# One ring of four raw weight buffers in the MLPs, loaded from SyncE three blocks ahead, and the third up tile in two single PSUM banks

## The chip, the cores and the metric

The kernel runs on one core of one Trainium2 chip. Its time is the device time of one execution, in microseconds; the figure that counts is the median of several runs. A core has five engines that work through their instructions in order and meet at semaphores: TensorE (PE in the profile; its weight loads are listed as PEld), VectorE (DVE), ScalarE (ACT), GpSimd (POOL) and SyncE (SP). Data lie in HBM, in the on-chip SBUF, and, for what TensorE writes, in the eight banks of PSUM. DMA transfers are issued by an engine (here ScalarE or SyncE) and carried by 16 DMA engines.

## What is computed

One inference step of a two-layer streaming encoder over 576 tokens (512 of a new stream and 64 of a running one), with a model width of 1024 and an MLP width of 4096. Layer 0 mixes tokens by causal pooling, layer 1 by sparse attention; each is followed by the same kind of MLP. Cut to what the change touches:

```python
def _rmsnorm(x, g):
    xf = x.astype(jnp.float32)
    xf = xf * lax.rsqrt(jnp.mean(xf * xf, axis=-1, keepdims=True) + EPS)
    return (xf * g.astype(jnp.float32)).astype(x.dtype)

def _mlp(h, w_up, w_down):
    u = jax.nn.relu(h @ w_up)
    return (u * u) @ w_down

...
for i in range(DEPTH):
    h = _rmsnorm(x, norm_mix[i])
    ...
    x = x + y.astype(x.dtype)
    x = x + _mlp(_rmsnorm(x, norm_mlp[i]), mlp_w_up[i], mlp_w_down[i])
```

## The kernel before

**Stages.** Four stages follow one another: the pooling mixer (about 0 to 47 us of the span), the first MLP (48 to 457), the attention (457 to 761) and the second MLP (761 to the end). Each opens its own pools of SBUF and PSUM tiles (`stage`, L65, with the buffer counts that the calls at the file's end give); a tile of a new stage waits until the old tiles at its place have been read.

**Activations and products.** The residual `x` is kept transposed, as 8 tiles of 128 features by 576 tokens. Every fp32 value is split into a high part and a rest, and a product takes three matmuls: high by high, high by rest, rest by high. A matmul has weights of 128x128 and 288 tokens, half of the 576. An up tile (`project`, L226 to L234) is 128 hidden features by 576 tokens: 8 weight slices x 3 x 2 halves = 48 matmuls into a tile of two PSUM banks (`psum("up")`, of which the stage has two, `ps=2`). Single banks come from `psum1`, of which there are four (`po=4`).

**Weights.** All weight blocks go in one fixed order, the list `jobs` (L130 on). The generator `made` (L170) takes the next job: a `block` is 128x1024 fp32 (512 KB), loaded by `load` (L123 to L126) into one of two tiles of the pool `raws`, from ScalarE's DMA queue, and split into two *units* of 128x512 (`split_unit`, L164 to L168): ScalarE casts the high part `wh` (L166), VectorE (GpSimd for the first tiles of an MLP) subtracts for the rest `wl` (L167). Units lie in a ring of six, and within the MLPs two more, every fourth one. `next_unit` (L200) hands the oldest one to the matmuls and keeps up to five made ahead.

**Down products.** The 4096 hidden features go in four chunks, `c` = 0 to 3. All four chunks of the first MLP and the first three of the second use Strassen-like products with 7 instead of 8 products per `Pair` (L359): two blocks of `w_down` (a `pair` job, loaded on ScalarE's queue at L183 into the two tiles of a pool of its own, `pairs`) give seven units, three of them sums that GpSimd makes (L186, L187, L191, L194). TensorE does seven products of 12 matmuls (L356), three (`opening`) into banks a, b and c, then four (`closing`) that go on in banks a, b, c and b. They are read out by ScalarE or VectorE (L379 to L383) and VectorE (L395), each of which adds a bank to `x`. A chunk has four pairs. Before the down products of a chunk the first up tile of the next one is made.

**The norm of an MLP.** `xs` is the unnormed input times the gain; the scale per token comes later. `norm.stats` (L254, matmuls `st` at L284) sums the squares over features, a chain of small operations on ScalarE and VectorE (L301 to L308) gives the inverse root, `norm.spread` (L259) makes a diagonal of it (L274, L277) and spreads it over partitions with matmuls `rb` (L264), which ScalarE copies to SBUF (L265). Then `activated` (L325) reads an up tile, clamps it and scales it (VectorE, L327), ScalarE squares it (L328), and `factors` (L335 to L348) makes the operands `u` of the Strassen products from each two tiles. The loop at L424 on calls it thus:

```python
pt = psum("up")
project(pt, w, xs)
todo.append((c, i, pt, us[c]))
if n == 0:
    norm.stats()
    continue
if n == 1:
    norm.spread()
for t in todo:
    finished(*t)
```

**Order.** Program order is the order of the calls; a scheduler then places instructions on each engine by priorities and dependences, and what it fixes is what the engines execute, in order. In the first MLP TensorE's order is tile, tile, `st`, `rb`, tile; in the second it is tile, `st`, tile, `rb`, tile. The end of the kernel (`last`, L450) and the attention are not touched; the attention ends with `x` plus the output product (L1118) and the second MLP's first up tile takes banks that this addition reads.

Of the kernel before, what the change touches and what calls it, by code (L numbers as in the profile page):

```python
# [16 lines left out]
P = 128  # L17
# [20 lines left out]
UNITS = 6  # L38
# [5 lines left out]
def pool_dsa_kernel(ctx: ExitStack, tc: tile.TileContext, a, o):  # L44
# [5 lines left out]
    weights = ctx.enter_context(tc.tile_pool(name="weights", bufs=UNITS))  # L50
    raws = ctx.enter_context(tc.tile_pool(name="raws", bufs=2))
# [71 lines left out]
    def load(src, n, queue):  # L123
        raw = raws.tile([P, 4 * 264], F32, tag="raw", name=uid("raw"))
        queue.dma_start(raw[:, :n], src)
        return raw  # L126
# [15 lines left out]
    jobs.extend(("block", a["w_in"][j], KT * P) for j in range(2))  # L142
    jobs.extend(("block", a["w_v"][j], 4 * 264) for j in range(2))
    jobs.extend(("block", a["w_in"][j], KT * P) for j in range(2, 15))
    for _ in range(2):
        jobs.extend(("block", a["w_o"][m], KT * P) for m in range(KT))
# [4 lines left out]
    def unit(n=512):  # L151

        extra = phase.get("more")
        count[0] += 1
        if extra and made_units[0] % 4 == 3:
            got = [extra.tile([P, 528], F32R, tag=t, bufs=2, name=uid(t)) for t in ("wh", "wl")]
        else:
            got = [weights.tile([P, 528], F32R, tag=t, name=uid(t)) for t in ("wh", "wl")]
        made_units[0] += 1
        return [t[:, :n] for t in got]  # L160

    made_units = [0]

    def split_unit(src, n=512):  # L164
        h, l = unit(n)
        act.copy(h, src)  # L166
        how["sub"].tensor_tensor(l, src, f32(h), ALU.subtract)  # L167
        return h, l  # L168

    def made():  # L170
# [1054 lines left out]
```

## Time and profile before

| | |
|---|---|
| median of 3 runs | 1180.39 us (1179.42 to 1181.02) |
| profiled execution | 1183.02 us, of which 1181.3 us are the span |
| mean granted clock of TensorE | 0.977 of full |
| raw up blocks, loads | 64 of 512 KB, 3.6 us median from issue to landing |
| DMA | 116.67 MB, 99 GB/s mean; ScalarE's queue 84.45 MB, SyncE's 30.90 MB |
| VectorE's splits (L167) | 139.6 + 101.3 + 70.2 us for raw, pair and sum units |
| GpSimd's sums of a pair | 37.4 + 38.7 + 40.4 + 43.0 us for 28 pairs |

The profile is of one execution. Busy shares are read per engine over the span; an engine's waits are listed by what came last before it went on. A tile name stands for all buffers of that name: `raw`, `pair` and `sum` are fp32 weights, `wh` and `wl` the split ones, `a`, `b`, `c` the banks of a pair, `up` those of an up tile.

### The profile page before, as it was taken

The numbers are of one execution on the slowest core, as the hardware profiler recorded it, in microseconds if no ns is written. First come the engines' busy times: TensorE is split into PE (matmuls) and PEld (weight loads), VectorE is DVE, ScalarE is ACT, GpSimd is POOL, SyncE is SP. The second block draws the span as 40 slices with busy tenths as digits, with TensorE's granted clock in tenths as the row PEclk, the third lists the DMA queues.
The fourth block names the chain that finished last, engine by engine and source line by source line (L and its number), as shares of the span: only waits on it lengthen the run. The fifth ranks groups of instructions, "written<-read, shape, count | busy, mean of one in ns | idle before, by whom it ended". The sixth has DMA issues, their size and how long they took to land.

```text
span 1181.3 us, 20612 instructions
## 1 busy us (share of the span) xinstructions
PE 1117.8 (95%) x8244; PEld 1096.1 (93%) x8244; DVE 811.7 (69%) x1478; ACT 529.9 (45%) x968; POOL 354.4 (30%) x274
## 2 busy tenths in 40 slices
PE   7989989999999999999979999899999999999995
PEld 7989989999999988899878999899989999999995
DVE  7756566666667687658999973856666776775434
ACT  6634334334434434434368665644344334434331
POOL 7700330140132064027675341100430330350002
PEclk8989999999999999999989999999999999999998
DMA  5312232233124125186552332422241233123212
GB/s 170 112 56 67 65 118 72 57 114 99 54 72 143 54 70 192 37 232 195 147 165 69 116 111 79 161 90 61 83 126 55 71 116 99 37 73 116 81 37 80
DMA packets 51151, 116.67 MB, mean 99 GB/s; under 512 B 9345, under 2 KB 22960, under 8 KB 51056
## 3 DMA queue, kind: packets, MB, share of 16 engines
q10 hardware_dynamic: 23184, 84.45, 23.1%
q1 hardware_dynamic: 27872, 30.90, 8.9%
q8 instruction: 65, 1.06, 0.4%
q14 instruction: 30, 0.25, 0.1%
HBM read 99.73 MB, written 13.25 MB: 96 GB/s over the span
## 4 chain that ended last, share of the span: by engine, by line
PE 59%; issue 14%; DVE 14%; POOL 6%; DMA 4%; ACT 3%; SPq 0%; DVEq 0%; ACTq 0%; POOLq 0%
PE up L234 33%; DVE wl L167 6%; PE dn L234 4%; PE b L356 3%; PE o L986 3%; DMA raw<-in_w_up 2%; PE wo L234 2%; PE a L356 2%; PE wa L234 2%; PE c L356 2%; PE sc L947 2%; PE pt L967 1%; POOL sum L194 1%; POOL sum L186 1%; POOL sum L187 1%
## 5 line engine op out<-in xcount | busy, mean ns | idle before, releaser
L234 PE MATMUL up<-xs,wh 128*128 128x288 f32 x2048 | 360.4, 298 | 7.3 <-DVE x L1118 3.4
L234 PEld LDWEIGHTS up<-xs,wh 128*128 128x128 f32 x2048 | 304.6, 191 | 8.8 <-ACT sq L251 4.8
L166 ACT CAST wh<-raw 128x512 fp32r<-128x512 f32 (+1 forms) x210 | 126.6, 619 | 226.1 <-PE up L234 90.8
L234 PE MATMUL up<-xs,wl 128*128 128x288 f32 x1024 | 222.1, 297 | 0.7 <-DVE wl L167 0.7
L167 DVE TENSOR_TENSOR wl<-raw,wh 128x512 fp32r<-128x512 f32 (+1 forms) x186 | 139.6, 756 | 95.2 <-ACT wh L166 93.5
L234 PEld LDWEIGHTS up<-xs,wl 128*128 128x128 f32 x1024 | 166.7, 190 | 1.1 <-DVE wl L167 1.1
L356 PE MATMUL b<-u,wh 128*128 128x288 f32 x672 | 139.1, 300 | 10.2 <-DVE x L395 8.1
L167 DVE TENSOR_TENSOR wl<-pair,wh 128x512 fp32r<-128x512 f32 x112 | 101.3, 910 | 35.9 <-ACT wh L166 35.3
L194 POOL TENSOR_TENSOR sum<-sum,pair 128x512 f32<-128x512 f32 x28 | 43.0, 1534 | 275.9 <-DVE wl L167 275.9
L356 PEld LDWEIGHTS b<-u,wh 128*128 128x128 f32 x672 | 108.1, 190 | 14.3 <-DVE x L395 10.4
L186 POOL TENSOR_TENSOR sum<-pair 128x512 f32<-128x512 f32 x28 | 37.4, 1337 | 274.1 <-DMA pair<-in_w_down 274.1
L166 ACT CAST wh<-sum 128x512 fp32r<-128x512 f32 x84 | 51.0, 620 | 150.4 <-POOL sum L187 44.1
L166 ACT CAST wh<-pair 128x512 fp32r<-128x512 f32 x112 | 68.0, 619 | 90.9 <-PE up L234 40.8
L356 PE MATMUL b<-u,wl 128*128 128x288 f32 x336 | 99.6, 299 | 2.4 <-DVE wl L167 2.3
L327 DVE SCALAR_TENSOR_TENSOR v<-up,rbm 128x576 f32<-128x576 f32 x64 | 48.2, 756 | 73.1 <-PE up L234 70.1
L356 PE MATMUL a<-u,wh 128*128 128x288 f32 x448 | 92.2, 297 | 2.6 <-DVE u L347 2.0
L356 PE MATMUL c<-u,wh 128*128 128x288 f32 x448 | 91.6, 296 | 2.6 <-DVE x L395 2.4
L167 DVE TENSOR_TENSOR wl<-sum,wh 128x512 fp32r<-128x512 f32 x84 | 70.2, 847 | 33.5 <-ACT wh L166 33.2
L234 PE MATMUL pj<-xs,wh 128*128 128x288 f32 x448 | 80.2, 296 | 0.0
L356 PEld LDWEIGHTS a<-u,wh 128*128 128x128 f32 x448 | 72.4, 189 | 3.4 <-DVE u L347 2.3
L356 PEld LDWEIGHTS c<-u,wh 128*128 128x128 f32 x448 | 71.7, 188 | 4.0 <-ACT wh L166 3.3
L234 PEld LDWEIGHTS pj<-xs,wh 128*128 128x128 f32 x448 | 67.3, 190 | 0.7
(229 smaller groups left out, 2218.7 us busy)
## 6 DMA issues: line engine op xcount, KB each, us to landing
raw<-in_w_up ACTq DMA_DIRECT2D x64, 512.0 KB, 3.6
pair<-in_w_down ACTq DMA_DIRECT2D x56, 512.0 KB, 3.6
raw<-in_w_o ACTq DMA_DIRECT2D x16, 512.0 KB, 3.6
raw<-in_w_in ACTq DMA_DIRECT2D x15, 512.0 KB, 4.7
q<-st SPq DMA_DIRECT2D x32, 144.0 KB, 2.6
q<-q SPq DMA_DIRECT2D x16, 256.0 KB, 2.9
raw<-in_w_down ACTq DMA_DIRECT2D x8, 512.0 KB, 3.6
x<-in_x SPq DMA_DIRECT2D x8, 288.0 KB, 6.1
```

The source lines that it names most:

```text
L166: act.copy(h, src)
L167: how["sub"].tensor_tensor(l, src, f32(h), ALU.subtract)
L186: pool.tensor_tensor(s1, a21, a22, ALU.add)
L187: pool.tensor_tensor(s2, s1, a11, ALU.add)
L194: pool.tensor_tensor(s2, s2, a12, ALU.add)
L234: pe.matmul(pt[:, h, :m], wt, xs[k][:, part, c:c + m], start=(k == 0 and i == 0), stop=(k == n - 1 and i == 2),)
L327: dve.scalar_tensor_tensor(v, pt[:, :, :HT], 0.0, halves(norm.rb), ALU.max, ALU.mult)
L356: pe.matmul(bank[:, :HT], wt, ut, start=first and j == 0 and i == 0, stop=last and j == 3 and i == 2, skip_group_check=True)
L947: pe.matmul(pt[:, hh, :nw], q[:, 2 * s + hh], ks[g][:, part, :nw], start=part == 0, stop=part == 1)
L967: pe.transpose(pp[:, c:c + P], pr[:, hh, kt * P:(kt + 1) * P], ident)
L986: pe.matmul(oc[:, 2 * s + hh], pT[:, c:c + P], V[:, kt, vs], start=kt == 0, stop=kt == i)
```

## The change

**One ring.** The pool `pairs` goes. Within an MLP all raw blocks, up and down, take tiles in turn from `raws` (two) and from a further pool of the stage (two), a ring of four. A pair's two blocks are two entries of the list (`even`, `odd`), and its sum a21 + a11 is made in place in the raw tile, as before in the pair's. The sums `s1`, `s2` have a pool of four of their own.

**Loads.** A new generator, `loaded`, issues the loads of up to three blocks before it gives out the first of them (one outside the MLPs). The MLPs' blocks (`up`, `even`, `odd`, `down`) are loaded from SyncE, the others (`w_in`, `w_v`, `w_o`) still from ScalarE.

**Units.** The ring of six and two stays for the MLPs' blocks; the others use the six.

**Third up tile.** `norm.stats` comes after the second tile, `norm.spread` after the third, and the three tiles are then finished together. Since the stage has two double tiles of PSUM, the third tile takes two single banks, and `activated` reads it with two operations of 288 tokens. In the changed program TensorE's order is, in both MLPs, tile, tile, `st`, tile (its matmuls alternating between the two banks), `rb`, tile.

The diff, cut to its core:

```diff
@@ -35,7 +35,10 @@
 NORM_STEPS = (5, 14, 17)
 PACE = (1, 2, 2)
 SLOTS = {"xs": 8, "a": 3, "b": 3, "c": 3, "d": 3, "e": 2}
-UNITS = 6
+UNITS = (6, 2)
+RAWS = (2, 2)
+MLP_BLOCKS = ("up", "even", "odd", "down")
+LOADS_AHEAD = {True: 3, False: 1}
 UP_ORDER = (0, 4, 1, 5, 2, 6, 3, 7)
 FACTORS = ("b11", "b22", "b21", "t1", "t2", "t3", "t4")
@@ -120,8 +123,21 @@
         def __getitem__(self, k):
             return self.t[k // 2][:, k % 2]
-    def load(src, n, queue):
-        raw = raws.tile([P, 4 * 264], F32, tag="raw", name=uid("raw"))
+    turns = {"raw": 0, "unit": 0}
+    def longer(what, sizes, mlp):
+        if not (mlp and "more" in phase):
+            return False
+        t, turns[what] = turns[what], turns[what] + 1
+        return t * sizes[1] // sum(sizes) != (t + 1) * sizes[1] // sum(sizes)
+    def raw_tile(mlp=False):
+        pool = phase["more"] if longer("raw", RAWS, mlp) else raws
+        return pool.tile([P, 4 * 264], F32, tag="raw", name=uid("raw"))
+    def load(src, n, queue, mlp=False):
+        raw = raw_tile(mlp)
         queue.dma_start(raw[:, :n], src)
         return raw
@@ -129,71 +145,71 @@
     def mlp_jobs(layer, strassen):
         for c in range(4):
-            ups = [("block", a["w_up"][layer, c * 8 + f], KT * P) for f in UP_ORDER]
+            ups = [("up", a["w_up"][layer, c * 8 + f], KT * P) for f in UP_ORDER]
             jobs.extend(ups[1:] if c else ups)
             if c < 3:
-                jobs.append(("block", a["w_up"][layer, (c + 1) * 8 + UP_ORDER[0]], KT * P))
+                jobs.append(("up", a["w_up"][layer, (c + 1) * 8 + UP_ORDER[0]], KT * P))
             if c < strassen:
-                jobs.extend(("pair", a["w_down"][layer, c, 2 * q], a["w_down"][layer, c, 2 * q + 1]) for q in range(KT // 2))
+                for m in range(KT):
+                    jobs.append(("odd" if m % 2 else "even", a["w_down"][layer, c, m], KT * P))
             else:
-                jobs.extend(("block", a["w_down"][layer, c, m], KT * P) for m in range(KT))
+                jobs.extend(("down", a["w_down"][layer, c, m], KT * P) for m in range(KT))
...
-    def unit(n=512):
...
+    def unit(n=512, mlp=False):
+        pool = phase["more"] if longer("unit", UNITS, mlp) else weights
+        return [pool.tile([P, 528], F32R, tag=t, name=uid(t))[:, :n] for t in ("wh", "wl")]
+    def split_unit(src, mlp):
+        h, l = unit(src.shape[1], mlp)
         act.copy(h, src)
         how["sub"].tensor_tensor(l, src, f32(h), ALU.subtract)
         return h, l
+    def loaded():
+        waiting = []
+        while jobs or waiting:
+            while jobs and len(waiting) < LOADS_AHEAD["more" in phase]:
+                kind, src, n = jobs.pop(0)
+                mlp = kind in MLP_BLOCKS
+                waiting.append((kind, load(src, n, nc.sync if mlp else act, mlp)[:, :n], mlp))
+            yield waiting.pop(0)
     def made():
-        while jobs:
-            kind, one, two = jobs.pop(0)
-            if kind == "block":
-                raw = load(one, two, act)
+        blocks = loaded()
+        for kind, raw, mlp in blocks:
+            if kind != "even":
+                n = raw.shape[1] // 2
                 for i in range(2):
-                    yield split_unit(raw[:, i * two // 2:(i + 1) * two // 2], two // 2)
+                    yield split_unit(raw[:, i * n:(i + 1) * n], mlp)
                 continue
-            r = [phase["pairs"].tile([P, KT * P], F32, tag="pair", bufs=2, name=uid("pair")) for _ in range(2)]
-            for t, src in zip(r, (one, two)):
-                act.dma_start(t, src)
-            a11, a12, a21, a22 = (t[:, i * 512:(i + 1) * 512] for t in r for i in range(2))
-            s1, s2 = (phase["pairs"].tile([P, 512], F32, tag="sum", bufs=4, name=uid("sum")) for _ in range(2))
+            a11, a12, a21, a22 = (t[:, i * 512:(i + 1) * 512] for t in (raw, next(blocks)[1]) for i in range(2))
+            s1, s2 = (phase["sums"].tile([P, 512], F32, tag="sum", name=uid("sum")) for _ in range(2))
             pool.tensor_tensor(s1, a21, a22, ALU.add)
             pool.tensor_tensor(s2, s1, a11, ALU.add)
-            yield split_unit(a11)
-            yield split_unit(s2)
-            yield split_unit(s1)
+            yield split_unit(a11, mlp)
+            yield split_unit(s2, mlp)
+            yield split_unit(s1, mlp)
             pool.tensor_tensor(a21, a21, a11, ALU.add)
-            yield split_unit(a12)
-            yield split_unit(a21)
+            yield split_unit(a12, mlp)
+            yield split_unit(a21, mlp)
             pool.tensor_tensor(s2, s2, a12, ALU.add)
-            yield split_unit(s2)
-            yield split_unit(a22)
+            yield split_unit(s2, mlp)
+            yield split_unit(a22, mlp)
     units = made()
@@ -232,7 +248,7 @@
             for i, (wt, part) in enumerate(((wh, 0), (wh, 1), (wl, 0))):
                 for h, (c, m) in enumerate(cols):
                     pe.matmul(
-                        pt[:, h, :m], wt, xs[k][:, part, c:c + m],
+                        pt[h][:, :m] if isinstance(pt, tuple) else pt[:, h, :m], wt, xs[k][:, part, c:c + m],
                         start=(k == 0 and i == 0), stop=(k == n - 1 and i == 2),
                     )
@@ -324,7 +340,11 @@
         def activated(pt, v):
-            dve.scalar_tensor_tensor(v, pt[:, :, :HT], 0.0, halves(norm.rb), ALU.max, ALU.mult)
+            if isinstance(pt, tuple):
+                for h in range(2):
+                    dve.scalar_tensor_tensor(v[:, h], pt[h][:, :HT], 0.0, halves(norm.rb)[:, h], ALU.max, ALU.mult)
+            else:
+                dve.scalar_tensor_tensor(v, pt[:, :, :HT], 0.0, halves(norm.rb), ALU.max, ALU.mult)
             act.activation(v, v, AF.Square)
         def plain(pt, u):
@@ -424,13 +444,15 @@
         for n, (c, i) in enumerate(steps):
             if i is not None:
                 w = next_block(sub=add if n < 2 else dve)
-                pt = psum("up")
+                pt = (psum1("up"), psum1("up")) if n == 2 else psum("up")
                 project(pt, w, xs)
                 todo.append((c, i, pt, us[c]))
                 if n == 0:
+                    continue
+                if n == 1:
                     norm.stats()
                     continue
-                if n == 1:
+                if n == 2:
                     norm.spread()
                 for t in todo:
                     finished(*t)
@@ -1120,11 +1142,11 @@
     x = Residual()
     with stage(slots=1, xs=1, tmps=6, ps=3, po=2):
         pool_mixer()
-    with stage(u=1, xs=1, acts=1, tmps=3, pairs=1, more=2, ps=2, po=4):
+    with stage(u=1, xs=1, acts=1, tmps=3, sums=4, more=2, ps=2, po=4):
         mlp(0, 1, 4, pool)
     with stage(slots=1, xs=1, cst2=1, tmps=6, ps=3, po=2):
         attention()
-    with stage(xs=1, u=1, acts=1, tmps=3, pairs=1, more=2, ps=2, po=4):
+    with stage(xs=1, u=1, acts=1, tmps=3, sums=4, more=2, ps=2, po=4):
         mlp(1, 3, 3, end=last)
 
```

More of the change, by code (lines that the diff above doesn't have):

```diff
@@ L131, in mlp_jobs @@
         for c in range(4):
-            ups = [("block", a["w_up"][layer, c * 8 + f], KT * P) for f in UP_ORDER]
+            ups = [("up", a["w_up"][layer, c * 8 + f], KT * P) for f in UP_ORDER]
             jobs.extend(ups[1:] if c else ups)
             if c < 3:
-                jobs.append(("block", a["w_up"][layer, (c + 1) * 8 + UP_ORDER[0]], KT * P))
+                jobs.append(("up", a["w_up"][layer, (c + 1) * 8 + UP_ORDER[0]], KT * P))
             if c < strassen:
-                jobs.extend(("pair", a["w_down"][layer, c, 2 * q], a["w_down"][layer, c, 2 * q + 1]) for q in range(KT // 2))
+                for m in range(KT):
+                    jobs.append(("odd" if m % 2 else "even", a["w_down"][layer, c, m], KT * P))
             else:
-                jobs.extend(("block", a["w_down"][layer, c, m], KT * P) for m in range(KT))
+                jobs.extend(("down", a["w_down"][layer, c, m], KT * P) for m in range(KT))
     mlp_jobs(0, 4)
-    jobs.extend(("block", a["w_in"][j], KT * P) for j in range(2))
-    jobs.extend(("block", a["w_v"][j], 4 * 264) for j in range(2))
-    jobs.extend(("block", a["w_in"][j], KT * P) for j in range(2, 15))
+    jobs.extend(("w_in", a["w_in"][j], KT * P) for j in range(2))
+    jobs.extend(("w_v", a["w_v"][j], 4 * 264) for j in range(2))
+    jobs.extend(("w_in", a["w_in"][j], KT * P) for j in range(2, 15))
     for _ in range(2):
-        jobs.extend(("block", a["w_o"][m], KT * P) for m in range(KT))
+        jobs.extend(("w_o", a["w_o"][m], KT * P) for m in range(KT))
     mlp_jobs(1, 3)
@@ L149, in pool_dsa_kernel @@
     how = {"sub": dve}
-    def unit(n=512):
[L153 to L165, printed above, removed]
+    def unit(n=512, mlp=False):
[3 more added lines that the diff above has]
+        h, l = unit(src.shape[1], mlp)
         act.copy(h, src)
@@ L811, in split_cache @@
             dve.tensor_copy(t[:, :, TP:], f32(new[:, :, TP:]))
-            raw = raws.tile([P, 4 * 264], F32, tag="raw", name=uid("raw"))
+            raw = raw_tile()
             nc.sync.dma_start(raw[:, :TP], src)
```

4 lines of the change are left out of this document (2 added, 2 removed).

## Prediction

> **What bounds the kernel now.** I read the page's busy row first, then the waits of TensorE, then the chain of work that ended last in the stretches where those waits lie, then a table by stage.
>
> ```profile
> PE 1117.8 (95%) x8244; PEld 1096.1 (93%) x8244; DVE 811.7 (69%) x1478; ACT 529.9 (45%) x968; POOL 354.4 (30%) x274
> ```
>
> TensorE is the bound: of a span of 1181.3 us it lacks only 63.5. Nothing in the change takes a matmul away, so all that it can win lies in those 63.5 us and in stretches at a lower clock. The profiled execution took 1183.02 us, 2.6 above the median of 1180.39; I sum savings on the profile and take them from the median.
>
> ```profile
> PE b L356 <- DVE x L395: 8.1, 8, 2.2
> PE rb L264 <- DVE diag L274: 4.8, 2, 2.7
> PE c L356 <- DVE x L395: 2.4, 3, 1.2
> PE a L356 <- DVE u L347: 2.0, 1, 2.0
> ```
>
> Columns: who waited for whom, us in total, times, the longest. The a, b and c rows are the down products of the MLPs; `x L395` is an accumulation that reads a PSUM bank, so TensorE waits there for a bank to come free. An add of 0.45 us isn't slow in itself; the chain says what it stood behind. It is that of the end of chunk 0 in the first MLP:
>
> ```profile
> 149.77 1.30 POOL sum L186
> 151.14 1.30 POOL sum L187
> ...
> 154.75 1.78 DVE wl L167
> 162.23 4.45 DMA raw<-in_w_up
> 167.03 0.45 DVE x L395
> ```
>
> A weight block is asked for at 162.23, one block ahead, and lands 4.45 us later; its split sits in VectorE's order ahead of the accumulation. So a late load becomes a held PSUM bank. Thirteen us earlier the same chain goes through GpSimd's sums of a pair of blocks. By stretch (start:end, us, then PE, PEld, DVE, ACT and POOL busy, clock, DMA share, GB/s): from the first down phase to the last of the first MLP, one undisturbed up phase, and from the first down phase to the third of the second MLP:
>
> ```profile
> 100.00:457.00 357.00, 343.56 (x2529) 338.20 (x2528) 245.40 (x373) 145.38 (x223) 97.24 (x72) 0.99 0.26 82
> 269.00:320.00 51.00, 51.00 (x386) 51.00 (x387) 34.33 (x52) 23.99 (x33) 1.30 (x1) 1.00 0.27 81
> 831.00:1070.00 239.00, 234.24 (x1749) 231.69 (x1748) 166.80 (x254) 95.90 (x150) 71.67 (x55) 1.00 0.27 84
> ```
>
> The up phase is full: 51.00/386 = 132 ns for a matmul, 6.3 us for an up tile of 48, 11.1 us for a pair of 84. So all that the long stretches lack, 13.44 and 4.76, 18.2 us in sum, they lack in the down phases. Of these 2.0 is the wait on `u L347`, the last factor of a chunk, which the change does not touch; 16.2 are open to it.
>
> **The change, part by part.**
>
> *Loads three blocks ahead from SyncE in a ring of four.* A load takes this long from issue to landing (KB each, median us):
>
> ```profile
> pair<-in_w_down ACTq DMA_DIRECT2D x56, 512.0 KB, 3.6
> ```
>
> In the changed program the two blocks of a pair are asked for when the pair before it begins to be split, about 11.1 us of TensorE's work ahead, and the up blocks behind the last pair wait only for the tiles of the pair before. 11.1 against 3.6 to 4.5 hides the transfer, and GpSimd's first two sums (2.6 us) fit behind it. GpSimd's order also has the next pair's sums ahead of the last sum of the pair at hand. I take as won the waits that follow directly from a load or a pair's first sums. Here they are, the idle time of TensorE in brackets:
>
> ```profile
> 144.11 0.37 PE L356 MATMUL c<-u,wh 128*128 128x288 f32 x1 [0.97 <-DVE x L395]
> 157.04 0.37 PE L356 MATMUL c<-u,wh 128*128 128x288 f32 x1 [1.17 <-DVE x L395]
> 167.53 0.41 PE L356 MATMUL b<-u,wh 128*128 128x288 f32 x1 [1.82 <-DVE x L395]
> 268.85 0.40 PE L356 MATMUL b<-u,wh 128*128 128x288 f32 x1 [2.20 <-DVE x L395]
> 366.73 0.40 PE L356 MATMUL b<-u,wh 128*128 128x288 f32 x1 [0.86 <-DVE x L395]
> 449.69 0.53 PE L356 MATMUL b<-u,wh 128*128 128x288 f32 x2 [1.05 <-ACT wh L166]
> 451.27 0.40 PE L356 MATMUL b<-u,wl 128*128 128x288 f32 x1 [1.05 <-DVE wl L167]
> 874.49 0.41 PE L356 MATMUL b<-u,wh 128*128 128x288 f32 x1 [1.63 <-DVE x L395]
> 971.85 0.40 PE L356 MATMUL b<-u,wh 128*128 128x288 f32 x1 [0.62 <-DVE x L395]
> ```
>
> Sum 11.4 us. The other 4.8 of the 16.2, small waits of 0.1 to 0.5, I leave standing. Bounds: 0 (nothing helps) to 16.2. Two of these places also cost clock, in the stretch that follows:
>
> ```profile
> 166.10:168.20 2.10, 0.67 (x5) 0.68 (x6) 2.10 (x4) 0.06 (x1) 0.46 (x1) 1.00 0.01 4
> 168.20:171.60 3.40, 3.40 (x16) 3.40 (x16) 2.04 (x4) 1.24 (x2) 0.00 (x0) 0.51 0.53 157
> 451.50:454.90 3.40, 3.40 (x16) 3.40 (x16) 3.40 (x6) 1.51 (x4) 3.27 (x3) 0.51 0.00 0
> ```
>
> After a stretch with 0.67 of 2.10 us busy the granted clock is 0.51 for 3.4 us, in which TensorE does 1.7 us of full work. If the waits go, 2 x 1.7 = 3.4 us go with them. The Trainium skill ("TensorE: Matmul & The Clock Gate", Why this matters for your kernels) sets the limit higher: no idle gap over about 3 us. By that page a gap of 1.82 would not drop the clock and the 3.4 would stay. The trace speaks against it here; the rule stands as a rival below.
>
> The issues themselves move from ScalarE's queue to SyncE's, at this price each:
>
> ```profile
> 162.23 0.33 ACTq L125 DMA_DIRECT2D raw<-in_w_up  x1
> ```
>
> ScalarE is 45% busy and was waiting at the places above, so I count nothing. In the MLPs SyncE has nothing else to issue that TensorE waits for; behind a load that waits for its tile stand only later loads, and at the end of the first MLP the attention's reads, which wait for `x L395` anyway.
>
> *The third up tile, and the norm after it.* In the first MLP the sums of squares follow the second tile, and the scale needs them at once:
>
> ```profile
> 65.80:76.10 10.30, 8.41 (x29) 7.33 (x30) 6.03 (x10) 4.69 (x7) 0.00 (x0) 0.50 0.12 47
> 66.31 2.29 PE L264 MATMUL rb<-diag,ones 128*128 128x288 f32 x4 [2.17 <-DVE diag L274]
> 69.97 1.30 PE L234 MATMUL up<-xs,wh 128*128 128x288 f32 x4 [1.37 <-DVE v L327]
> 771.00:782.00 11.00, 9.71 (x71) 9.12 (x70) 5.08 (x14) 3.61 (x9) 0.00 (x0) 1.00 0.36 117
> 779.58 1.13 PE L264 MATMUL rb<-diag,ones 128*128 128x288 f32 x4
> ```
>
> The second MLP already has a tile between the two, and its rows (the last two) are the model: no wait before `rb`, the four matmuls in 1.13 us, clock 1.00. Putting 6.3 us of matmuls into a gap of 2.17 saves the 2.17; `rb` at full clock saves 2.29 - 1.13 = 1.16; and the matmuls from 69.97 to 76.10 run at 0.50, so 3.06 of those 6.13 us come back. Sum 6.4 us. The wait of 1.37 for `v L327` stays in both MLPs, since tiles four and five still take the banks of tiles one and two. The changed program reads the third tile with two operations of 288 columns; an add of that size took 0.45, two of them 0.9, for one tile per MLP, and all of it is hidden since the next product is 6.3 us long. Bounds: if the clock drops all the same, 2.17 to 3.33; for the second MLP 0, as its rows hold no such wait.
>
> *The two entries.* The second MLP starts late, because a load issued at 757.24 holds VectorE:
>
> ```profile
> 764.08 0.76 PE L234 MATMUL up<-xs,wh 128*128 128x288 f32 x4 [3.40 <-DVE x L1118]
> 742.00:761.00 19.00, 18.68 (x128) 18.42 (x126) 18.90 (x27) 12.77 (x22) 5.15 (x3) 1.00 0.43 132
> 743.90 0.68 DVE L167 TENSOR_TENSOR wl<-raw,wh 128x512 fp32r<-128x512 f32 x1
> 743.99 1.74 POOL L186 TENSOR_TENSOR sum<-pair 128x512 f32<-128x512 f32 x1 [24.69 <-DMA pair<-in_w_down]
> 746.28 1.79 DVE L167 TENSOR_TENSOR wl<-raw,wh 128x512 fp32r<-128x512 f32 x1
> 755.22 1.28 DVE L167 TENSOR_TENSOR wl<-raw,wh 128x512 fp32r<-128x512 f32 x2
> ```
>
> In the changed program that load waits for the split that ends at 756.50 (the last row) and not for ScalarE's turn at 757.24, 0.7 us earlier, and GpSimd's three sums, beside which a split took 1.79 instead of 0.68 us (about 3 us lost in all), come later. Against that, up to four more splits (4 x 0.68 = 2.7) are made ahead in a stretch where VectorE is busy 18.90 of 19.00. Net +0.7; bounds -2.7 to +3.4. At the first MLP's start ScalarE makes a few casts earlier among the mixer's scalings: -0.3, bounds -1.5 to 0. Into the attention the first two blocks now wait for tiles of the last pair; they are several split units ahead, so 0, and a load of 3.6 if that cover fails.
>
> **Sum:** 11.4 + 3.4 + 6.4 + 0.7 - 0.3 = 21.6 us. 1180.4 - 21.6 = **1158.8 us** (on the profiled execution 1183.0 - 21.6 = 1161.4).
>
> **The rivals.**
>
> *Half of the waits stay.* VectorE works in order, and GpSimd's adds still slow its splits; banks may be held for that reason with the load long there. For it: the wait of 1.17 at 157.04 has a split of 1.78 just ahead. Against it: those at chunk ends follow loads alone. Then 5.7 + 1.7 + 6.4 + 0 = 13.8: 1166.6, with 1164 to 1171 around it.
>
> *The ring does not do what it says.* Four tiles serve pairs and up blocks alike; if the tiles come free so late that loads are again only just in time, the norm alone is left: 1180.4 - 6.4 = 1174. If that too is eaten at the entries (-2.7, -1.5, -3.6), it is no change. Against it: a tile comes free with the last split of its pair, and the next load has a pair's time.
>
> *The clock does not hang on these gaps.* Two short gaps may stand beside drops that have another cause and stay. Then 21.6 - 3.4 - 3.1 - 1.2 = 13.9: 1166.5. Against it: the norm of the second MLP, with no such gap, kept 1.00. This is the case that the page's rule of 3 us would give.
>
> *Slower: the sums that run ahead meet VectorE all the time.* In a pair VectorE has 7 splits of 0.68 and some 7 accumulations of 0.45: 7.9 us beside 11.1 of TensorE, so 3.2 us of room. Today GpSimd's first sums often run while VectorE waits for the late load. Ahead of time, all four adds of a pair run beside its work. An add beside VectorE's work cost it 1.79 - 0.68 = 1.1 us; four cost 4.4, 1.2 more than the room; over 28 pairs 34 us. It decides from a loss of 3.2 us per pair on: 1158.8 + 34 = 1193. Against it: VectorE is busy 72% of the pair, so about 2.9 adds' worth is met, 3.2 us: just the room. The Trainium skill ("SBUF — State Buffer", Who interferes with whom) says that the port pair which the two share is an exclusive lock and the loser blocks for a whole instruction; worked out from the add of 1.74 above, an estimate, that would be up to 7 us per pair. The trace shows 1.1 for one.
>
> **How the numbers follow.** Forecast as summed (1152 to 1164): 0.50. Half of the waits stay: 0.20. Clock rule: 0.06. Ring late: 0.10, of which 0.04 no change. Slower by VectorE: 0.14, of which 0.01 within the bound. A difference of 0.2% (2.4 us) is about what a measurement of this kernel can tell from no change. So faster 0.82, same 0.05, slower 0.13. The low end is all open terms won: 16.2 + 3.4 + 6.4 + 3.4 = 29.4, 1151; the high end takes in the norm alone, 1174, and an entry lost at 1.5 to 2.7 beside it: 1176. Left out are the slower case and the last of the ring's.
>
> **What would show it.** Right: no `PE rb <- DVE diag` wait in the first MLP and clock 1.00 through its first six tiles; chunk ends without waits for `x L395` behind a load; TensorE's idle time near 50 us (63.5 less 11.4, 2.2 and 0.4). Half right: the same waits, now with a split of over 1 us ahead. Wrong: VectorE's splits in the pairs at a mean over 1.1 us, waits of b and c on `x L395` growing in mid phase; or SyncE's queue waiting for tiles while ScalarE waits for loads; or a new wait where the second MLP starts.

## The result, and the profile after

The changed kernel takes 1142.33 us (median of 4 runs, 1141.16 to 1144.35) against 1180.7 before (4 runs): a ratio of 0.9677 with a 95% interval of 0.9658 to 0.9696, 38 us faster. The forecast was 1158.8 us with a range down to 1151: the sign was right, the size was not, for the gain is 1.8 times the 21.6 us of the sum. The profiled execution took 1141.55 us, its span 1139.8; against the profiled span of before that is 41.5 us, of which some 3 are the spread of single runs (a second profile of the changed kernel has a span of 1142.0).

The page's first row, and those of TensorE's waits (who waited for whom, us, times, longest) in the changed kernel that bear on the change. Lines have moved: `L356` is now `L376`, `L395` is `L415`, `L327` is `L347`, `L264` is `L280`, the split `L167` is `L176`, and GpSimd's sums `L186`, `L194` are `L202`, `L210`:

```profile
PE 1097.8 (96%) x8244; PEld 1083.8 (95%) x8244; DVE 839.9 (74%) x1480; ACT 532.8 (47%) x968; POOL 365.5 (32%) x274
```

```profile
PE ix L901 <- ACT rl L909: 5.1, 3, 2.0
PE up L250 <- DVE v L347: 2.6, 2, 1.3
PE a L376 <- DVE u L367: 2.0, 1, 2.0
PE up L250 <- DVE x L1140: 1.1, 1, 1.1
PE c L376 <- DVE x L415: 0.8, 1, 0.8
PE b L376 <- DVE u L368: 0.6, 1, 0.6
```

The 10.5 us of waits of b and c on `x L395` are down to 0.8. What is left in the MLPs is in the main the wait for the scaled up tile (2.6) and for a chunk's last factors (2.0 and 0.6), the first two of which the prediction had left standing. But TensorE's busy time itself fell by 20.0 us with the same 8244 matmuls, and that was not all clock. Down phases of chunks 1 and 2 of the first MLP, before and after (start:end, us, PE, PEld, DVE, ACT, POOL busy, clock, DMA share, GB/s):

```profile
220.00:269.00 49.00, 46.26 (x343) 45.20 (x342) 32.84 (x55) 16.07 (x28) 20.46 (x15) 1.00 0.31 95
320.00:367.00 47.00, 45.56 (x338) 44.52 (x337) 31.24 (x55) 15.63 (x27) 20.55 (x15) 1.00 0.30 93
```

```profile
207.00:250.00 43.00, 43.00 (x328) 43.00 (x327) 34.22 (x55) 17.16 (x28) 12.56 (x9) 1.00 0.32 108
302.00:345.00 43.00, 43.00 (x327) 43.00 (x326) 34.86 (x56) 17.16 (x28) 12.54 (x9) 1.00 0.36 109
```

After, the down phase is full: 43.00 us busy of 43.00, 131.1 ns for a matmul. Before, it was 46.26/343 = 134.9 ns, at a clock of 1.00. So besides the idle time there was a loss inside the busy time. It isn't a slower pace: from one start to the next a matmul takes 132 ns (median) in both traces. The loss stands at the waits. A matmul is listed with 0.29 us (the profile models its end) although the next one starts 0.13 us after it, so the first 0.16 us of every wait are counted as busy; here is the longest wait of chunk 1, before:

```profile
266.36 0.29 PE L234 MATMUL up<-xs,wl 128*128 128x288 f32 x1
268.85 0.54 PE L356 MATMUL b<-u,wh 128*128 128x288 f32 x2 [2.20 <-DVE x L395]
```

From start to start this is 2.49 us, 2.36 more than the usual 0.13, of which 2.20 are listed as idle; and the two matmuls behind it take 0.54 us instead of 0.42. Over the seven down phases such losses come to some 9 us (26.8 gained, less 3.4 of clock, less the idle time, which fell from 18.2 to 3.8), which the count of idle time never showed. Note also GpSimd's column: it does 9 operations in the stretch instead of 15; the other sums are made before the down phase begins.

Where the 41.5 us of the two profiled spans came from, by the start of the same matmul in both traces (us, minus is faster). A chunk counts from its first down product to the next chunk's, with the up phase between, which is full in both; chunk 3 counts to its last down product.

| stretch | measured | forecast |
|---|---|---|
| up to the first MLP's first up tile | +1.0 | +0.3 |
| the norm and first chunk's up tiles, first MLP | -6.3 | -6.4 |
| first MLP, chunks 0, 1, 2, 3 | -7.5, -4.0, -2.5, -4.6 | |
| second MLP, chunks 0, 1, 2 | -3.2, -2.2, -2.9 | |
| all these down phases, clock included | -26.8 | -14.8 |
| attention | -5.5 | 0 |
| start of the second MLP, up to its first down phase | -3.9 | -0.7 |

The expectations below were written with 28.1 for the down phases and 4.1 for the attention. They took chunk 3 up to the attention's first `pj` matmul, which the scheduler has moved ahead of ten others in the changed program; those 1.3 us belong to the attention.

### The profile page after: what moved, and what is told of

Same layout as the page of the kernel before. It is cut to its first block, busy times and chain, and to the rows that moved or that the text cites. A ratio compares the mean times of both kernels' runs of the same rounds, so it can differ in the third digit from the quotient of the medians.

```text
span 1139.8 us, 20796 instructions
## 1 busy us (share of the span) xinstructions
PE 1097.8 (96%) x8244; PEld 1083.8 (95%) x8244; DVE 839.9 (74%) x1480; ACT 532.8 (47%) x968; POOL 365.5 (32%) x274
## 4 chain that ended last, share of the span: by engine, by line
PE 86%; DVE 9%; ACT 2%; issue 2%; DMA 0%; DVEq 0%; SPq 0%; ACTq 0%
PE up L250 36%; PE b L376 11%; PE c L376 7%; PE a L376 7%; PE pj L250 5%; PE dn L250 4%; PE o L1008 3%; PE wo L250 2%; DVE wl L176 2%; PE wa L250 2%; PE sc L969 2%; PE pt L989 1%; PE v L809 1%; DVE work L933 1%; PE pb L741 1%
## 5 line engine op out<-in xcount | busy, mean ns | idle before, releaser
L250 PE MATMUL up<-xs,wh 128*128 128x288 f32 x2048 | 356.0, 296 | 5.3 <-DVE v L347 2.6
L175 ACT CAST wh<-raw 128x512 fp32r<-128x512 f32 (+1 forms) x322 | 197.7, 620 | 307.9 <-PE up L250 124.1
L250 PEld LDWEIGHTS up<-xs,wh 128*128 128x128 f32 x2048 | 300.4, 189 | 6.6 <-DVE v L347 3.5
L176 DVE TENSOR_TENSOR wl<-raw,wh 128x512 fp32r<-128x512 f32 (+1 forms) x298 | 226.4, 762 | 78.7 <-ACT wh L175 73.1
L202 POOL TENSOR_TENSOR sum<-raw 128x512 f32<-128x512 f32 x28 | 40.3, 1440 | 457.2 <-DMA raw<-in_w_down 442.2
L376 PE MATMUL b<-u,wh 128*128 128x288 f32 x672 | 135.5, 295 | 0.8 <-DVE u L368 0.6
L376 PEld LDWEIGHTS b<-u,wh 128*128 128x128 f32 x672 | 107.4, 188 | 1.3 <-DVE u L368 0.8
L376 PE MATMUL b<-u,wl 128*128 128x288 f32 x336 | 98.3, 295 | 0.0
L347 DVE SCALAR_TENSOR_TENSOR v<-up,rbm 128x576 f32<-128x576 f32 x62 | 46.6, 755 | 64.9 <-PE up L250 64.2
L376 PE MATMUL a<-u,wh 128*128 128x288 f32 x448 | 92.0, 295 | 2.0 <-DVE u L367 2.0
L376 PE MATMUL c<-u,wh 128*128 128x288 f32 x448 | 91.1, 295 | 1.0 <-DVE x L415 0.8
L176 DVE TENSOR_TENSOR wl<-sum,wh 128x512 fp32r<-128x512 f32 x84 | 84.9, 1011 | 3.0 <-ACT wh L175 0.7
L376 PEld LDWEIGHTS a<-u,wh 128*128 128x128 f32 x448 | 72.2, 188 | 2.3 <-DVE u L367 2.3
L376 PEld LDWEIGHTS c<-u,wh 128*128 128x128 f32 x448 | 71.8, 188 | 1.4 <-DVE x L415 1.1
L376 PE MATMUL a<-u,wl 128*128 128x288 f32 x224 | 66.1, 295 | 0.0
L376 PE MATMUL c<-u,wl 128*128 128x288 f32 x224 | 66.0, 295 | 0.0
L348 ACT ACTIVATE v<-v 128x576 f32<-128x576 f32 x64 | 43.9, 687 | 46.7 <-DVE v L347 45.2
```

Source lines behind the costliest of these rows:

```text
L202: pool.tensor_tensor(s1, a21, a22, ALU.add)
L250: pe.matmul(pt[h][:, :m] if isinstance(pt, tuple) else pt[:, h, :m], wt, xs[k][:, part, c:c + m], start=(k == 0 and i == 0), stop=(k == n ...
L347: dve.scalar_tensor_tensor(v, pt[:, :, :HT], 0.0, halves(norm.rb), ALU.max, ALU.mult)
L348: act.activation(v, v, AF.Square)
L376: pe.matmul(bank[:, :HT], wt, ut, start=first and j == 0 and i == 0, stop=last and j == 3 and i == 2, skip_group_check=True)
```

## The experiments

Ratios are against runs of the kernel before on the same chip; the intervals are at 95%. "Changed" is 0.9677.

**The third up tile alone.** The kernel before with `psum1("up")` twice for the third tile, `norm.stats` and `norm.spread` one tile later, and `activated` for a pair of banks; nothing else of the diff.

> The kernel before with the third up tile and the moved norm alone; weight tiles and loads as before. The traces of before and after, laid side by side at each tile, put 6.3 us of the gain between the first and the fourth up tile of the first MLP, 28.1 in the seven down phases, 4.1 in the attention, 4.0 at the second MLP's start, and 1.0 lost at the first MLP's start. Theory: the third tile makes the 6.3 and nothing else: 1174. Rival: it also makes the second MLP's start early, 4.0 more: 1170.

Measured 1173.45 us, ratio 0.9947 [0.9921, 0.9973]. The theory's 1174 holds. In the trace the first MLP gains 6.6 us up to its first down phase; the down phases together move by 1.6 us.

**Everything but the third up tile.**

```diff
-                pt = (psum1("up"), psum1("up")) if n == 2 else psum("up")
+                pt = psum("up")
...
                 if n == 0:
-                    continue
-                if n == 1:
                     norm.stats()
                     continue
-                if n == 2:
+                if n == 1:
                     norm.spread()
```

> The changed kernel with the norm and the up tiles as before: ring of four, three loads ahead, SyncE's queue. If the parts add: 1142.3 + 6.3 = 1148.6. Rival: in this program TensorE's order has 31 of the second tile's 48 matmuls between the sums of squares and the spreading, 4.1 us where the gap was 2.17, so the ring alone already removes the gap and its half clock, and the third tile adds nothing: 1142 to 1144.

> The ring without the third up tile's change, once more. If the third tile adds nothing on top of the ring (TensorE's order in the first MLP already has 31 matmuls between the sums of squares and the spreading): within 1.5 us of the changed kernel. If the parts add: 6 us above it.

Measured 1144.0 us, 0.9706 [0.9676, 0.9736], and in the second run, beside the changed kernel on one chip, 1144.6 us, 0.9689 [0.9671, 0.9708] against 0.9674 [0.9657, 0.9691] (1143.31 us) for the changed kernel.

> The changed kernel once more, beside the next two on the same chip, for differences of a few tenths of a per cent: 1142 to 1144.

So the parts do not add: the third tile is worth some 6 us alone and about 1.5 on top of the ring, which the intervals don't tell from nothing. The trace of this kernel says why, in the first MLP's norm:

```profile
61.60 1.16 PE L300 MATMUL st<-ones,s 128*128 128x2 f32 x10
66.88 1.13 PE L280 MATMUL rb<-diag,ones 128*128 128x288 f32 x4
69.38 0.77 PE L250 MATMUL up<-xs,wh 128*128 128x288 f32 x4 [1.37 <-DVE v L347]
```

Between the sums of squares and the spreading lie 31 matmuls, 4.1 us, with no wait and at full clock. In this program the scheduler had already put `st` into the second tile; the gap of 2.17 us that the prediction closed with the third tile was closed without it.

**The queue and the lead.** The changed kernel with the MLPs' loads on ScalarE's queue:

```diff
-                waiting.append((kind, load(src, n, nc.sync if mlp else act, mlp)[:, :n], mlp))
+                waiting.append((kind, load(src, n, act, mlp)[:, :n], mlp))
```

> The changed kernel with the MLPs' loads issued by ScalarE instead of SyncE, everything else as changed. Theory of the lead: a load issued three blocks ahead is early on any queue: 1142 to 1145. Rival, the queue: a load that waits for its tile in ScalarE's order holds back the casts behind it, and 128 issues of 0.33 us are 42 us of ScalarE's time: a third or more of the 28 us of the down phases is lost, 1152 to 1170.

and the changed kernel with `LOADS_AHEAD = {True: 1, False: 1}`:

> The changed kernel with one load ahead instead of three, still on SyncE and in the ring of four. Theory of the lead: most of the 28 us of the down phases go back, 1160 to 1170. Rival: SyncE waits for nothing but the tile, and a load's issue there does not stand behind casts, so that the queue alone gives the lead: 1142 to 1147.

Measured 1145.16 us, 0.9723 [0.9698, 0.9749], and 1143.7 us, 0.971 [0.9683, 0.9737]. In both, the down phases gain what they gain in the changed kernel, chunk for chunk within 0.2 us but for the last chunk of each MLP (up to 0.7). The theory of the lead, which was the prediction's, expected 1160 to 1170 for one load ahead: it falls, though the ratios leave room for a loss of some 4 us outside the down phases. Either one could stand in for the other, so both were taken away at once:

> The changed kernel with one load ahead and ScalarE's queue, both at once: of the loads only the shared ring of four is left. Shared ring: 1143 to 1148, with the down phases as full as in the changed kernel (43.00 of 43.00 us). Rival, that lead and queue stand in for each other: 1160 to 1172.

Measured 1144.88 us, 0.9709 [0.9665, 0.9753]. The down phases again gain as much as in the changed kernel (27.3 us): they need neither lead nor queue. And the queue alone, on the kernel before (both `act.dma_start` of a pair and the MLPs' `load` on `nc.sync`):

> The kernel before with the MLPs' loads issued by SyncE, its tiles and everything else as they were. Shared ring: the down phases stay as they were, 1176 to 1181 (at most the second MLP's start gains 2). Rival, the queue: 1160 or less.

Measured 1180.82 us, 1.0005 [0.998, 1.003]. No difference.

**The tiles.** The changed kernel, with the same four raw tiles, but two kept for pairs and two for the rest:

```diff
-    def raw_tile(mlp=False):
-        pool = phase["more"] if longer("raw", RAWS, mlp) else raws
+    def raw_tile(pair=False):
+        pool = phase["more"] if pair else raws
```

> The changed kernel (three loads ahead, SyncE, third tile), but the four raw tiles are not one ring: two are kept for the pairs' blocks and two for the others, as in the kernel before. New theory, the shared ring: what held the down phases was that a pair's two tiles were the only ones, so that the next pair's loads, and GpSimd's sums behind them, could not begin until the last of seven units of the pair at hand was split. Then most of the 28 us goes back, however early the loads are asked for: 1162 to 1172. Rival, lead or queue (either of them enough by itself): 1142 to 1146.

Measured 1163.92 us, 0.9868 [0.9828, 0.9908]: three loads ahead from SyncE and the third tile, and still 21 us of the gain gone. By stage, this profile's down phases gain 4.2 us instead of 26.8; the norm (7.0), the attention (5.4) and the second MLP's start (4.4) keep their gains. The cause is in the tiles. Take the first sum of the fourth pair of chunk 1, which can't start before that pair's two blocks have landed. The first rows are the start of the chunk's first product `a` and then that sum, in the kernel before, in this one, and in the changed one:

```profile
219.88 0.43 PE L356 MATMUL a<-u,wh 128*128 128x288 f32 x2
250.71 1.29 POOL L186 TENSOR_TENSOR sum<-pair 128x512 f32<-128x512 f32 x1 [6.12 <-DMA pair<-in_w_down]
```

```profile
208.47 0.42 PE L376 MATMUL a<-u,wh 128*128 128x288 f32 x2
237.38 1.29 POOL L202 TENSOR_TENSOR sum<-raw 128x512 f32<-128x512 f32 x1 [5.87 <-DMA raw<-in_w_down]
```

```profile
207.11 0.42 PE L376 MATMUL a<-u,wh 128*128 128x288 f32 x2
224.62 1.30 POOL L202 TENSOR_TENSOR sum<-raw 128x512 f32<-128x512 f32 x1 [5.15 <-DMA raw<-in_w_down]
```

The sum comes 30.8 us into the chunk before, 28.9 with the tiles apart, 17.5 with the ring. The fourth pair's products begin after three pairs of 11.1 us, at 33: at 31 and 29 its units are made just as they are needed, at 17.5 they lie ready. What held the load shows in the kernel before. The last unit of the third pair is split, and the load of the fourth pair's second block is issued as that split ends (246.40 + 0.68 = 247.08); it lands as the sum above begins:

```profile
246.40 0.68 DVE L167 TENSOR_TENSOR wl<-pair,wh 128x512 fp32r<-128x512 f32 x1
247.11 0.33 ACTq L183 DMA_DIRECT2D pair<-in_w_down  x1
```

With two tiles for the pairs, the load of a pair's second block can't start before the last of the seven units of the pair ahead of it is split, no matter how early it is asked for; in the ring the two tiles that the up blocks leave idle in a down phase take the next pair. So each pair comes one pair earlier: in the ring the first sum of chunk 1's second pair is made at 187.59, 20 us ahead of the chunk's first product, and with the tiles apart at 210.28, 2 us behind it. GpSimd's own waits show the same thing, apart above and changed below:

```profile
POOL sum L210 <- DVE wl L176: 285.3, 25, 69.8
POOL sum L202 <- DMA raw<-in_w_down: 231.5, 26, 18.1
```

```profile
POOL sum L202 <- DMA raw<-in_w_down: 442.2, 26, 67.9
...
POOL sum L210 <- DVE wl L176: 39.8, 18, 3.5
```

Apart, most of the 285 us are spent in the up phases (34 of them ahead of chunk 1), at the last sum of the next chunk's first pair (L210, which waits for a split of the same pair), with nothing of the second pair to do; in the ring GpSimd has the second pair's sums done by then and waits for the third pair's load. TensorE's waits with the tiles apart are the old ones:

```profile
PE b L376 <- DVE x L415: 9.0, 11, 2.0
```

How many tiles does it take? A ring of three, `RAWS = (2, 1)`:

> The changed kernel with a ring of three raw tiles instead of four. Shared ring: the next pair's first block can load early, but its second waits for the pair at hand, and GpSimd's first sum needs both of that second block's halves; the down phases lose half to three quarters of their 28 us: 1156 to 1165. Rival, one free tile is enough: 1142 to 1147.

Measured 1146.18 us, 0.9697 [0.968, 0.9714], beside 0.9674 for four. My expectation of half to three quarters lost was wrong and the rival right: one free tile is nearly enough, with three raw tiles in all where the kernel before has four. Its chunk 1 is as full as with four, 21.3 us from the first product to the fourth pair's first sum; a little is lost in other chunks:

```profile
209.33 0.42 PE L376 MATMUL a<-u,wh 128*128 128x288 f32 x2
```

```profile
230.64 1.29 POOL L202 TENSOR_TENSOR sum<-raw 128x512 f32<-128x512 f32 x1 [8.11 <-DMA raw<-in_w_down]
```

```profile
PE c L376 <- DVE x L403: 2.8, 3, 1.8
```

Last, the shared tiles and nothing else: one load ahead, ScalarE's queue, norm and up tiles as before.

> The ring of four alone: one load ahead, ScalarE's queue, norm and up tiles as before. Its order in the first MLP has one matmul between the sums of squares and the spreading, as good as none. If the shared tiles make the 28 us of the down phases and the attention's 4, and the norm's 6 need work between: 1146 to 1150, the down phases as full as in the changed kernel. Rival, tiles and one of lead, queue or third tile work only together: 1158 or more.

Measured 1149.73 us, 0.9744 [0.972, 0.9767], within the expectation; its down phase of chunk 0 is full, its norm is not:

```profile
112.00:155.00 43.00, 43.00 (x327) 42.88 (x326) 33.98 (x52) 18.70 (x33) 13.19 (x9) 1.00 0.29 88
```

```profile
67.38 1.59 PE L280 MATMUL rb<-diag,ones 128*128 128x288 f32 x4 [2.40 <-DVE diag L290]
```

```profile
68.10:74.90 6.80, 5.43 (x22) 4.64 (x21) 4.91 (x8) 4.21 (x6) 0.00 (x0) 0.50 0.09 36
```

In this kernel only one matmul lies between `st` and `rb`, and the gap (2.40) and the half clock are back. So of the 38 us the shared tiles alone make 30. The third tile on top of them, which is the run with one load ahead on ScalarE's queue, makes some 4 more (0.9744 to 0.9709); the last 4, up to the changed kernel, lie within the intervals. Summed over the seven down phases, the profiles gain 26.8 us in the changed kernel, 27.2 with the ring alone, 23.8 with a ring of three and 4.2 with the tiles apart; SyncE's queue alone loses 1.7.

**The slower rival's price.** GpSimd's first sum of each pair, made three times:

```diff
-            pool.tensor_tensor(s1, a21, a22, ALU.add)
+            for _ in range(3):
+                pool.tensor_tensor(s1, a21, a22, ALU.add)
```

> The changed kernel with GpSimd's first sum of every pair made three times over (the same sum, two repeats too many). This puts a price on the slower rival of the prediction: in the down phases VectorE is now busy 34.2 of 43.0 us, 8.8 spare, 2.3 for a pair. Two more adds beside VectorE's work, at 1.1 us each, take 2.2: if that is the price and splits may run late by what is spare, 1142 to 1148. If an add blocks VectorE for its whole 1.44 us, 0.6 too much for each of 28 pairs: 1158 or more.

Measured 1156.28 us, 0.9799 [0.976, 0.9838], between the two: 1.2% above the changed kernel, 14 us, 0.5 for each of 28 pairs. In the profile all of it is lost in the down phases. The price of an add doesn't follow from this, for the run does two things at once. First, VectorE is held: its busy time grew from 839.9 to 880.2 us, 0.7 us for each of the 56 adds, and TensorE waits for accumulations again (lines are one further in this run):

```profile
L176 DVE TENSOR_TENSOR wl<-sum,wh 128x512 fp32r<-128x512 f32 x84 | 94.9, 1132 | 12.3 <-ACT wh L175 11.7
```

```profile
PE b L377 <- DVE x L416: 6.0, 8, 1.6
```

Second, GpSimd's other sums come later, and ScalarE's casts wait for them, 64 us in all where the changed kernel has 3.8. The longest row here and there:

```profile
ACT wh L175 <- POOL sum L204: 33.5, 13, 5.7
```

```profile
ACT wh L175 <- POOL sum L203: 2.4, 1, 2.4
```

How the 14 us divide between the two is open. What an add does to a single split can be read directly, here in the changed kernel:

```profile
213.73 1.30 POOL L210 TENSOR_TENSOR sum<-sum,raw 128x512 f32<-128x512 f32 x1 [0.63 <-DVE wl L176]
```

```profile
213.94 1.64 DVE L176 TENSOR_TENSOR wl<-sum,wh 128x512 fp32r<-128x512 f32 x1
215.50 0.68 DVE L176 TENSOR_TENSOR wl<-raw,wh 128x512 fp32r<-128x512 f32 x1
```

The split begins while the add has 1.09 us left and takes 0.96 longer than the next one, which has no add beside it; of the 89 splits in the traces of before, after and this run that begin with over 0.25 us of one add left, 88 are longer by what is left of it, less some 0.13 us. That agrees with the Trainium skill ("SBUF — State Buffer", Who interferes with whom), by which the port pair that the two engines share is an exclusive lock. So the mechanism of this rival is real: an add can cost VectorE up to nearly its whole length, and the added ones cost 0.7 us on average. In the changed kernel's down phases TensorE loses nothing by it (43.00 of 43.00 us busy); with two adds more per pair it does.

**The attention.** In every kernel with `loaded`, TensorE's order at the attention's start has other products between `st` and `rb`, and the wait of 2.66 us with the halved clock behind it is gone. In the kernel before, the same by hand:

```diff
-        rb = norm.spread()
-
         wv = [next_block(), next_block()]
         for i in range(5):
             n = P if i < 4 else TS
+            if i == 2:
+                rb = norm.spread()
             pt = psum1("v")
```

> The kernel before with one thing moved, in the attention: the spreading of the norm is called after the first two v products (48 matmuls) instead of ahead of them. In the kernel before TensorE waits there 2.66 us for the diagonal, and the clock halves for 3.4 us right behind it; in every kernel with the ring TensorE's order has other matmuls between the sums of squares and the spreading, and the wait is gone. Theory: this order is what the attention's 4.1 us come from: 2.7 + 1.7 = 4.4 us faster than before, 1176. Rival: the wait goes over to the index products behind it, and the time stays: 1179 to 1181.

Measured 1180.65 us, 1.0007 [0.9993, 1.0021]: no difference. The wait did go (2.66 to 0.34), but the index products behind it wait longer for their transposed queries (1.7 us before) and for ScalarE (2.7 before):

```profile
PE ix L879 <- DMA qi<-qi: 3.8, 2, 3.4
PE ix L879 <- ACT rl L887: 3.8, 1, 3.8
```

The theory that this order alone makes the attention's 4 us falls. Over the profiles of the ring kernels the attention is between 3.0 and 5.5 us faster than before; what makes it is not settled.

**A version that beats both.** The spreading called from within the third tile, through `project`'s `between`:

```diff
-                project(pt, w, xs)
+                project(pt, w, xs, midway(norm) if n == 2 else iter(()))
...
-                if n == 2:
-                    norm.spread()
...
+        def midway(norm):
+            for k in range(KT):
+                if k == 5:
+                    norm.spread()
+                yield
```

> The changed kernel with the spreading called after five of the third tile's eight weight slices instead of after the tile, so that TensorE's order has 38 of the 48 matmuls before it and 10 behind it. In the changed kernel TensorE waits 1.28 us in each MLP for the first read of an up tile behind the spreading; ten matmuls are 1.3 us. If that wait is only the chain of copy and read behind the spreading, both waits go: 2.5 us faster than the changed kernel, 1140. Rival: VectorE has three tiles to read at once and the wait only moves to the next tile: no difference.

Measured 1139.78 us, 0.9645 [0.9629, 0.9661], 3.5 us below the changed kernel on the same chip. The two waits of 1.3 us for `v L347` are gone from the waits of TensorE; the ten matmuls behind the spreading cover the copy and the first read, and the next tile's first row (72.94) has no wait:

```profile
70.52 1.13 PE L280 MATMUL rb<-diag,ones 128*128 128x288 f32 x4
...
72.94 0.80 PE L250 MATMUL up<-xs,wh 128*128 128x288 f32 x4
```

## Why the prediction was wrong

**What bounds the kernel.** Right that TensorE is the bound and that the down phases are where it is held. The limit "all that it can win lies in those 63.5 us and in stretches at a lower clock" was wrong: each wait of TensorE hides its first 0.16 us in the busy time and the matmuls right behind it are listed longer, some 9 us in all. The sign of it was at hand: 51.00/386 is 132 ns in the full up phase, and 343.56 us for 2529 matmuls, in the same fence, is 135.8; that comparison was not made.

**The loads.** This is the step that failed. The prediction's term was "Loads three blocks ahead from SyncE in a ring of four"; it argued from how early a load is asked for, and took as won the waits that follow directly from a load or a pair's first sums, 11.4 us and 3.4 of clock. The runs: with lead and queue, each or both, undone, the ratio is 0.971 to 0.972 beside 0.968 and the down phases gain all the same; the queue alone gives nothing (1.0005); with the tiles apart the lead keeps 16 us of the 38, of which 4 are in the down phases. The cause is the sharing of the four tiles. The prediction had the fact at hand (a pair's two tiles were the only ones) and read the wait as a late issue and not as a full buffer.

The size failed with it: 26.8 us were measured against 14.8. A pair that is ready a whole pair early takes away not only the longest waits but the just-in-time running of the stage: most of the 4.8 us of small waits that were left standing went too, and so did the part of every wait that the idle time doesn't show. On the two profiles the sum falls 19.9 us short: 12.0 in the down phases, 5.5 in the attention and 3.2 at the second MLP's start, less 0.8 at the first MLP's start and in the norm.

**The clock.** Right. The drops at 168 and 451 us are gone, and no stretch from 53 to 571 us is below full clock. Where a gap of 2.40 us comes back (the bare ring), a stretch of 6.8 us at 0.50 comes with it. By the Trainium skill ("TensorE: Matmul & The Clock Gate", Why this matters for your kernels) a gap under 3 us would be harmless; here it is not, so that rival is out. Length alone doesn't decide, though: in the kernel before, 1.82 us of waiting at 167.53 was followed by 3.4 us at 0.51, and 2.20 us at 268.85 by a clock of 1.00.

**The norm.** Right in size (6.3 against 6.4) for this pair of profiles, and alone (6 us in the third-tile run), but wrong as a term of a sum: with the ring and its loads the scheduler's own instruction order made most of it (6.0 and 7.6 us in two profiles without the third tile, 2.5 with the bare ring).

**The entries and the attention.** The second MLP's start gained 3.9 where 0.7 was taken, above the bound of 3.4. Of this, 2.3 are the shorter wait for `x L1118` (3.40 to 1.13), and most of the rest is a stretch at half clock behind the long wait, which no term held and which is gone after:

```profile
765.60:768.90 3.30, 3.30 (x16) 3.30 (x15) 2.13 (x4) 1.45 (x3) 0.00 (x0) 0.50 0.41 149
```

This start gains 1.3 to 5.1 us in each of the ten profiles whose kernel loads the MLPs' blocks from SyncE (4.2 with the queue alone) and 0 to 2.2 in the five others with ScalarE's queue. So the queue seems to make much of it, though the whole time of the run with the queue alone doesn't show it. The first MLP's start lost 1.0 where 0.3 was taken; single profiles differ there by as much (0.7 in the attention's run, whose code is as before up to there). The attention's gain of 5.5 was in no term: the text took that order as unchanged, and it was not.

**The rivals.** That half of the waits stay, or that the ring comes too late: no, in the changed kernel; with the tiles apart the time (1163.9) is near the first of them (1166.6), as most of the waits are back. Slower by VectorE: not in this change. The splits took 139.6 + 101.3 + 70.2 = 311.1 us before and 226.4 + 84.9 = 311.3 after, though the adds do run beside its work; VectorE's extra 28 us are in other operations: the four on `t` that make the factors went from 61.7 to 81.7 us, as 33 of them now meet an operation of GpSimd instead of 14 (1.4 us each, against 0.45 alone). But there is little room, as the tripled sum shows.

## What to carry to other kernels

When a load is late, ask first what its issue waits for: if it is the tile, neither another queue nor an earlier request helps, and one more tile, borrowed from a use that is idle in that stage, may be worth more than both. Compare the busy time per instruction between a full stretch and the stretch in question, since part of every wait can sit inside the busy time. And parts of a change that close the same gap do not add, above all where a scheduler reorders around each of them.

## What the hardware showed besides

A VectorE split of two on-chip operands that begins during a GpSimd add waits for what is left of the add, less some 0.13 us: 1.64 us instead of 0.68 with 1.09 left. A gap of 2.40 us, with 1.59 us of the four `rb` matmuls and another 1.37 behind it, halved TensorE's clock for 6.8 us.
